# The first MLP in seven block products with transposed output, with one running sum and a reordered last group in both MLPs

## The chip, the cores and the metric

The kernel runs on one core of a Trainium2 chip. TensorE (PE) multiplies, VectorE (DVE), ScalarE (ACT) and GpSimd (POOL) work elementwise, SyncE (SP) and POOL issue the DMAs used here. The metric is the device time of one execution in microseconds; the median of several runs counts.

## The reference

A trunk of two layers over 512 tokens of 1024 channels, all float32. Layer 0 mixes tokens with a gated DeltaNet, layer 1 with a Conformer convolution. Each layer then attends into a fixed memory of 256 rows and applies an MLP:

```python
h = h + memory_cross_attention(rms_norm(h, xa_norm[layer]), ...)
h = h + sq_relu_mlp(rms_norm(h, mlp_norm[layer]), mlp_w_up[layer], mlp_w_down[layer])

def sq_relu_mlp(h, w_up, w_down):
    return jnp.square(jax.nn.relu(h @ w_up)) @ w_down
```

`w_up` is 1024 x 4096 and `w_down` 4096 x 1024. The result goes through a last RMSNorm.

## The kernel before

**Precision.** Every matmul operand is held as two parts in a fast 32-bit type: a rounded head and the remainder. A product of two such operands takes three matmuls (head x head, head x remainder, remainder x head). For weights, ACT writes the head `wh` from the loaded tile and DVE (in a few places POOL) the remainder `wl`, in `wsplit`; for activations `split` or `Norm.parts` does so. `Norm.add(t, h)` takes tile t of the residual: ACT scales it to `xh`, DVE makes `xl`, ACT squares it, POOL (for the last tile DVE) adds the squares. `norm.stat` sums the squares over the channels with two matmuls; ACT's root and DVE's reciprocal of 3.35 us give `rb`, by which the results are scaled when they are read from PSUM.

**Layout.** The residual is held transposed: 8 tiles of 128 channels x 512 tokens. `proj` computes 128 output channels for all tokens: 8 blocks of the contraction, three matmuls each, so 24 matmuls of 128 x 512, with the weights stationary.

**First MLP (`mlp`).** The 4096 hidden channels are taken in four groups of 1024. A group has 8 up projections and 8 down projections of 24 matmuls, in the order of `MLP_ORDER`. Each down result is added by DVE to the residual; in the last group this sum also reorders the tokens (`by_phase`, `phased`: token 4t+s goes to place s*128+t, as the convolution wants them), and `nxt.add` prepares the tile for the Conformer's norm at once. `mid`, called ahead of the last group, prepares the memory for layer 1 (`mem_gain`) and loads convolution taps.

**Second MLP (`mlp7`).** The down product of a group is a product of 2 x 2 blocks (halves of the tokens, halves of the hidden channels, halves of the output), and is done in seven block products instead of eight. The activations' blocks and their combinations (`early`, `late`: "11", "R3", "S1", "12", "R2", "S4", "22") are stationary and the weights' blocks move, so the result comes out with tokens on the partitions. The combined weight blocks are made by DMA: T3 and T1 are loaded and added to by accumulating DMAs on POOL's queue, T1's buffer (`T7`, of the three buffers `fs`) becomes T2 and later T4 by a further accumulation after each has been split (`after7`). Each product is 24 matmuls: 2 halves of 128 tokens, 4 blocks of the contraction, three matmuls. `evict` adds the results by DVE to eight accumulators (2 token halves x 2 output halves x 2), which in the first group have been filled with the turned residual by `turn` (32 PE transposes). Two more, "m" and "b", hold sums that belong to several outputs, and are given to them in the last group. `final` applies the last norm and writes the output.

**What sets the order.** The program is written in the order of the stages; a scheduler that knows durations then places instructions in each engine's queue, also earlier than they were written where buffers allow. Every engine works through its queue in order. `order`, `loads` and `need` plan the weights: each half weight tile (128 x 1024) is loaded by SP some units ahead (`wnext`: `NRAW` + 1, and two more from shortly ahead of the second MLP on) into six buffers `raw`, and split up to three units ahead (`NW`). 69 slots of 128 x 512 (`NSLOT`) hold the activations, 8 PSUM banks the results, 6 buffers `cv` the convolutions' inputs, three buffers `fs` the DeltaNet's solver, the convolution's inputs and the blocks T1.

**The Conformer's beginning.** `pw_mm` runs 16 projections (pairs m, half 0 and 1); the norm's statistics stand in the second of them, after its second contraction block. `pw_ev` then applies the gate. The convolution of pair 0 runs on ACT and POOL (`pool_conv`), of pairs 1 to 4 on DVE (`dve_conv`), of 5 to 7 on PE. Layer 1's memory projections fill PE beside them; POOL also splits some of these weights.

Of the kernel before, what the change touches and what calls it, by code (L numbers as in the profile page):

```python
# [14 lines left out]
P = 128  # L15
# [22 lines left out]
def tile_trunk(ctx, tc, xT, memT, x_d, mem_d, prm_d, adt_d, bdw_d, tap_d, fin_d, w_ab, w_kq, w_v, w_z, w_dno, w_pw1, w_pw2,  # L38
# [131 lines left out]
    def plan_mlp(layer):  # L170
        for kind, g in MLP_ORDER:
            for i in range(4):
                plan((kind, layer, g * 4 + i), (w_up if kind == "up" else w_dn)[layer, g * 4 + i])

    base7, sums7 = {}, set()
# [4 lines left out]
    def plan_mlp7(layer):  # L180
        for g in range(4):
            for i in range(4):
                plan(("up", layer, g * 4 + i), w_up[layer, g * 4 + i])
            n, base7["u", g] = len(loads), len(order)
            for b, h in LOADS7:
                if b == "T1":
                    sums7.add(len(loads))
                loads.append([block(layer, g, c, h) for c in PARTS7.get(b, [b])])
            for u in range(14):
                order.append((("dn7", g), u))  # L190
                bh = (ORDER7[u // 2][1], u % 2)
                need.append(n + LOADS7.index(bh) if bh in LOADS7 else need[-1])

# [9 lines left out]
    plan_mlp(0)  # L203
# [31 lines left out]
    def wsplit():  # L235
# [5 lines left out]
        raw = combos7(1, i, hf) if kind == "dn7" else ws["raw"].pop(need[u])  # L241
# [13 lines left out]
        if kind == "dn7":  # L255
            after7(1, i, hf)
# [13 lines left out]
    def combos7(layer, g, u):  # L270
        name, h = ORDER7[u // 2][1], u % 2
        if name in ("T2", "T4"):
            return T7[h]
        t = ws["raw"].pop(need[u + base7["u", g]])
        if name == "T1":
            T7[h] = t
        return t

    def after7(layer, g, u):
        name, h = ORDER7[u // 2][1], u % 2  # L280
        if name in ("T1", "T2"):
# [664 lines left out]

    def xattn(layer, norm, hres, nxt):
# [67 lines left out]
        def o_ev(m, ps):  # L1015
            hn = slot(s="h")
            tt(dve, hn, ps, hres[m], ALU.add)
# [38 lines left out]
    def mlp(layer, norm, hres, nxt, mid):  # L1056
        xs = norm.xs
        hid = {}
        cur = list(hres)
        st = {"first": []}  # L1060

        def up_ev(g, i, ps):
# [4 lines left out]
            hid.setdefault(g, []).append(split(u, "u"))  # L1067

        for kind, g in MLP_ORDER:
            if (kind, g) == ("dn", 3):  # L1070
                mid()
            for i in range(8):
                w = wnext((kind, layer, g * 4 + i // 2), i % 2)
                ps = psum(kind)
                if kind == "up":
                    proj(w, xs, ps, inside={1: norm.stat} if (g, i) == (0, 1) else None)
                    if g == 0 and i < 2:
                        st["first"].append(ps)
                        if i == 1:
                            for j in range(2):  # L1080
                                up_ev(0, j, st["first"][j])
                    else:
                        up_ev(g, i, ps)
                else:
                    proj(w, hid[g], ps)
                    hn = slot(s="h")
                    if g == 3:
                        tt(dve, by_phase(hn), phased(ps), phased(cur[i]), ALU.add)
                        nxt.add(i, hn)
                    else:  # L1090
                        tt(dve, hn, ps, cur[i], ALU.add)
                    cur[i] = hn
        return cur

    def phased(t):
        return t.rearrange("p (t s) -> p s t", s=4)  # L1100

    def by_phase(t):
        return t.rearrange("p (s t) -> p s t", s=4)
# [11 lines left out]
    def conformer(norm, hres, nxt):  # L1115
# [409 lines left out]
    h = mlp(0, n2, h, n3, lambda: (mem_gain(1, 0), mem_gain(1, 1), taps(NTAP)))  # L1525
    n4 = Norm("xa_norm1")
    h = conformer(n3, h, n4)
# [3 lines left out]

    def mlp7(layer, norm, hres):
        xs = norm.xs
        acc, first = {}, []
        gt = []

        def turn(i):
            n, m, c = i // 4, i // 2 % 2, i % 2
            ps, a = psum("hT"), slot(s="acc")
            for j in range(4):  # L1540
                pe.transpose(ps[:, j * P:(j + 1) * P], hres[4 * m + j][:, n * 256 + c * P:n * 256 + c * P + P], ident)
            act.copy(a, ps)
            acc[n, m, c] = a

        def up_ev(ps):
            t = slot(s="rl")
            stt(t, ps, 0.0, norm.rb, ALU.max, ALU.mult)
            u = slot(s="u2")
            act.activation(u, t, AF.Square)
            return u  # L1550

        def pair(t):
            return [t[0][:, 0:256], t[1][:, 0:256]], [t[0][:, 256:512], t[1][:, 256:512]]

        def early(o, u0):
            tt(dve, u0[:, 256:512], u0[:, 256:512], u0[:, 0:256], ALU.subtract)
            o["11"], o["R3"] = pair(split(u0, "a"))

        def late(o, u0, u1):
            x, y, r = slot(s="s12"), slot(s="s4"), slot(F32R, "s4")  # L1560
            tt(dve, x[:, 256:512], u1[:, 256:512], u0[:, 256:512], ALU.subtract)
            tt(dve, x[:, 0:256], u0[:, 0:256], x[:, 256:512], ALU.subtract)
            o["S1"], o["R2"] = pair(split(x, "s"))
            o["12"], o["22"] = pair(split(u1, "a"))
            tt(dve, y[:, 0:256], u1[:, 0:256], x[:, 256:512], ALU.subtract)
            act.copy(r[:, 0:256], y[:, 0:256])
            tt(dve, r[:, 256:512], y[:, 0:256], r[:, 0:256].bitcast(F32), ALU.subtract)
            o["S4"] = [r[:, 0:256], r[:, 256:512]]

        def dn7(g, ops):  # L1570
            bank = {}

            def part(left, w, ps, c, h, opens):
                for kk in range(2):
                    k, s = 2 * h + kk, slice(kk * 512, kk * 512 + 512)
                    xh, xl = [t[:, c * P:(c + 1) * P] for t in ops[k][left]]
                    pe.matmul(ps, xh, w[0][:, s], start=opens and k == 0, stop=False, skip_group_check=True)  # L1577
                    pe.matmul(ps, xl, w[0][:, s], start=False, stop=False, skip_group_check=True)  # L1578
                    pe.matmul(ps, xh, w[1][:, s], start=False, stop=k == 3, skip_group_check=True)  # L1579

            def product(i):
                left, right, key, opens = ORDER7[i]
                if opens:
                    bank[key] = [psum("dn") for _ in range(2)]
                ws_ = [wnext(("dn7", g), 2 * i)]
                if (g, i) == (3, 6):
                    ws_.append(wnext(("dn7", g), 13))
                    todo = [(0, 0), (0, 1), (1, 0), (1, 1)]
                else:
                    todo = [(0, 0), (1, 0), (0, 1), (1, 1)]  # L1590
                for c, h in todo:
                    if h == len(ws_):
                        ws_.append(wnext(("dn7", g), 2 * i + 1))
                    part(left, ws_[h], bank[key][c], c, h, opens)
                    if h == 1:
                        evict(right, c, bank[key][c])

            def into(key, c, ps, op=ALU.add):
                k = key + (c,)
                if k not in acc:  # L1600
                    acc[k] = slot(s="acc")
                    act.copy(acc[k], ps)
                else:
                    tt(dve, acc[k], acc[k], ps, op)
                return acc[k]

            def evict(right, c, ps):
                last = g == 3
                if right == "11":
                    m = into(("m",), c, ps)  # L1610
                    if last:
                        into((0, 0), c, m)
                        into(("b",), c, m, ALU.subtract)
                elif right == "T3":
                    into((0, 1), c, ps, ALU.subtract)
                elif right == "T1":
                    into((1, 1), c, ps)
                elif right == "21":
# [217 lines left out]
```

## Time and profile before

| | us |
|---|---|
| median of 3 runs | 1485.57 (1485.07 to 1485.91) |
| profiled execution | 1487.96 |
| its span | 1486.0 |
| first MLP, first up matmul to the Conformer's first matmul | 475.17 to 823.82 |
| second MLP, first up matmul to PE's end | 1145.16 to 1475.85 |
| PE's end to the end of the span | 10.15 |

The page gives the busy time of each engine and the chain of work that ended last. A table of stretches gives each engine's busy time in a window of the span. A row of the timeline has start, duration, engine, line, operation, output and inputs, and in brackets how long the engine stood idle before it and what ended that. Matmuls overlap, so the spacing of their starts is their price, not their duration. A group row has the count, then the busy time and the mean in ns of one, then the idle time before and its releasers. An operation that goes through a helper has the helper's line (`L69` is `tt`, `L72` is `stt`, `L78` is `ts`), so the tile's name tells more than the line.

### The profile page before, as it was taken

The numbers are of one execution on the slowest core, as the hardware profiler recorded it, in microseconds if no ns is written. First come the engines' busy times: TensorE is split into PE (matmuls) and PEld (weight loads), VectorE is DVE, ScalarE is ACT, GpSimd is POOL, SyncE is SP. The second block draws the span as 40 slices with busy tenths as digits, with TensorE's granted clock in tenths as the row PEclk, the third lists the DMA queues.
The fourth block names the chain that finished last, engine by engine and source line by source line (L and its number), as shares of the span: only waits on it lengthen the run. The fifth ranks groups of instructions, "written<-read, shape, count | busy, mean of one in ns | idle before, by whom it ended". The sixth has DMA issues, their size and how long they took to land.

```text
span 1486.0 us, 19375 instructions
## 1 busy us (share of the span) xinstructions
PE 1472.0 (99%) x7362; PEld 1241.1 (84%) x7362; DVE 986.7 (66%) x1468; ACT 729.0 (49%) x1262; POOL 240.2 (16%) x255
## 2 busy tenths in 40 slices
PE   9999999999999999999999999999999999999997
PEld 7888889988888888888888889988888888888885
DVE  5889888867555543443436699984645766767677
ACT  6766865655444432332314555464444554434344
POOL 1411310103112000000002388302112000000000
PEclk9999999999999999999999999999999999999999
DMA  7232123432213332223224524652203467575634
GB/s 269 93 114 72 58 87 126 142 115 97 73 34 109 99 100 95 91 98 100 99 99 156 174 96 135 192 178 93 86 29 113 114 170 178 140 193 140 186 99 113
DMA packets 55821, 176.63 MB, mean 119 GB/s; under 512 B 6961, under 2 KB 9265, under 8 KB 55729
## 3 DMA queue, kind: packets, MB, share of 16 engines
q1 hardware_dynamic: 50688, 158.10, 32.0%
q0 software_dynamic: 4608, 16.78, 6.6%
q8 instruction: 58, 0.95, 0.3%
q10 hardware_dynamic: 432, 0.52, 0.1%
q14 instruction: 35, 0.28, 0.1%
HBM read 172.49 MB, written 2.10 MB: 117 GB/s over the span
## 4 chain that ended last, share of the span: by engine, by line
PE 94%; DVE 3%; ACT 2%; issue 1%; DMA 1%; POOL 0%; SPq 0%; DVEq 0%
PE up L288 8%; PE up L287 8%; PE up L286 8%; PE dn L287 4%; PE dn L288 4%; PE dn L286 4%; PE dn L1578 3%; PE dn L1579 3%; PE dn L1577 3%; PE pw L288 3%; PE pw L287 3%; PE pw L286 3%; PE h L286 3%; PE h L287 2%; PE h L288 2%; PE xo L287 2%
## 5 line engine op out<-in xcount | busy, mean ns | idle before, releaser
L245 ACT CAST wh<-raw 128x1024 fp32r<-128x1024 f32 x255 | 267.7, 1051 | 498.1 <-PE up L287 133.7
L69 DVE TENSOR_TENSOR wl<-raw,wh 128x1024 fp32r<-128x1024 f32 (+1 forms) x246 | 303.7, 1236 | 93.7 <-ACT wh L245 87.6
L286 PE MATMUL up<-xh,wh 128*128 128x512 f32 x512 | 199.7, 390 | 0.0
L288 PE MATMUL up<-xh,wl 128*128 128x512 f32 x512 | 199.3, 389 | 0.0
L287 PE MATMUL up<-xl,wh 128*128 128x512 f32 x512 | 199.2, 389 | 0.0
L69 POOL TENSOR_TENSOR sq<-sq,sq 128x512 f32<-128x512 f32 x30 | 49.3, 1643 | 468.0 <-ACT sq L379 457.7
L72 DVE SCALAR_TENSOR_TENSOR rl<-up,rb 128x512 f32<-128x512 f32 x64 | 44.2, 691 | 106.0 <-PE up L288 105.9
L287 PEld LDWEIGHTS up<-xl,wh 128*128 128x128 f32 x512 | 96.1, 188 | 19.9
L286 PEld LDWEIGHTS up<-xh,wh 128*128 128x128 f32 x512 | 96.1, 188 | 19.9
L288 PEld LDWEIGHTS up<-xh,wl 128*128 128x128 f32 x512 | 96.1, 188 | 19.9
L286 PE MATMUL dn<-uh,wh 128*128 128x512 f32 x256 | 99.6, 389 | 0.0
L287 PE MATMUL dn<-ul,wh 128*128 128x512 f32 x256 | 99.6, 389 | 0.0
L288 PE MATMUL dn<-uh,wl 128*128 128x512 f32 x256 | 99.6, 389 | 0.0
L69 DVE TENSOR_TENSOR h<-dn,h 128x512 f32<-128x512 f32 x32 | 25.2, 788 | 91.5 <-PE dn L288 91.5
L1192 DVE SCALAR_TENSOR_TENSOR ca<-x,prm,ca 128x512 f32<-128x512 f32 x112 | 82.3, 753 | 3.6 <-ACT ca L1189 1.3
L286 PE MATMUL h<-xh,wh 128*128 128x512 f32 x184 | 73.7, 400 | 0.0
L288 PE MATMUL h<-xh,wl 128*128 128x512 f32 x184 | 71.9, 391 | 0.0
L287 PE MATMUL h<-xl,wh 128*128 128x512 f32 x184 | 71.7, 390 | 0.0
L286 PEld LDWEIGHTS dn<-uh,wh 128*128 128x128 f32 x256 | 48.0, 188 | 10.1
L287 PEld LDWEIGHTS dn<-ul,wh 128*128 128x128 f32 x256 | 48.0, 188 | 9.9
L288 PEld LDWEIGHTS dn<-uh,wl 128*128 128x128 f32 x256 | 48.0, 188 | 9.9
L72 DVE SCALAR_TENSOR_TENSOR cva<-cv,prm,cva 128x512 f32<-128x512 f32 x60 | 48.2, 830 | 11.4 <-POOL cva L69 10.3
(392 smaller groups left out, 3488.5 us busy)
## 6 DMA issues: line engine op xcount, KB each, us to landing
raw<-w_up SPq DMA_DIRECT2D x64, 512.0 KB, 3.5
raw<-w_dn SPq DMA_DIRECT2D x64, 512.0 KB, 3.5
raw<-w_pw SPq DMA_DIRECT2D x24, 512.0 KB, 3.6
t<-w_dn POOLq DMA_DIRECT2D x24, 512.0 KB, 5.6
raw<-w_k SPq DMA_DIRECT2D x16, 512.0 KB, 3.6
raw<-w_vv SPq DMA_DIRECT2D x16, 512.0 KB, 3.9
raw<-w_q SPq DMA_DIRECT2D x16, 512.0 KB, 3.4
raw<-w_o SPq DMA_DIRECT2D x16, 512.0 KB, 3.6
```

The costliest lines, as they stand in the source:

```text
L69: return e.tensor_tensor(out=o, in0=a, in1=b, op=op)
L72: return dve.scalar_tensor_tensor(out=o, in0=a, scalar=s, in1=b, op0=op0, op1=op1)
L245: ins = [act.copy(h, raw)]
L286: pe.matmul(ps, wh, xh, start=first, stop=False)
L287: pe.matmul(ps, wh, xl, start=False, stop=False)
L288: pe.matmul(ps, wl, xh, start=False, stop=last)
L1192: first["tap"] = dve.scalar_tensor_tensor(out=a, in0=src, scalar=w, in1=a, op0=ALU.mult, op1=ALU.add)
L1577: pe.matmul(ps, xh, w[0][:, s], start=opens and k == 0, stop=False, skip_group_check=True)
L1578: pe.matmul(ps, xl, w[0][:, s], start=False, stop=False, skip_group_check=True)
L1579: pe.matmul(ps, xh, w[1][:, s], start=False, stop=k == 3, skip_group_check=True)
```

## The change

- `mlp` is gone; `mlp7` serves both layers. In layer 0 it takes no `turn`: its accumulators start from the first result that reaches them (an ACT copy, negated where the result is to be subtracted), and the residual is added at the end. `outs` transposes the accumulators back, four output tiles with 16 PE transposes, adds the residual on DVE and calls `nxt.add`. Tiles 0 to 3 are done ahead of the last product of the last group, tiles 4 to 7 from inside the Conformer's first projection (`rest`).
- `pw_mm` does the first pair of projections in halves of the contraction: first half of projection 0, `rest`, first half of projection 1, second half of 0, second half of 1, with `norm.stat` in the last.
- The token order is changed in `o_ev` of layer 0's attention, so that the whole first MLP runs on reordered tokens.
- "m" and "b" become one running sum "p"; product "21" accumulates in the PSUM banks that product "11" opened, so that five opened pairs of banks become four.
- The last group of both layers runs in the order of `LAST7`: T2 directly after T1, and T2 is then loaded anew in three parts instead of being made from T1. Its buffer becomes T4.
- `BLOCKS7`, and with it the output halves, change places. Six of the ten accumulators (`ACC_CV`) lie in the `cv` buffers.
- Weights are loaded two units further ahead for all `up` and `dn7` units.

```diff
-LOADS7 = [(_b, _h) for _b in ("11", "T3", "T1", "21", "22") for _h in range(2)]
...
+            loads7 = [(o[1], h) for o in order7(g) if o[1] != "T4" and (g == 3 or o[1] != "T2") for h in range(2)]
...
-        while ws["load"] <= need[min(i + NRAW + 1 + 2 * (i > base7["u", 0] - 8), len(order) - 1)]:
+        while ws["load"] <= need[min(i + NRAW + 1 + 2 * (order[i][0][0] in ("up", "dn7")), len(order) - 1)]:
...
-            tt(dve, hn, ps, hres[m], ALU.add)
+            if layer == 0:
+                tt(dve, by_phase(hn), phased(ps), phased(hres[m]), ALU.add)
+            else:
+                tt(dve, hn, ps, hres[m], ALU.add)
...
+            def product(i):
+                if (layer, g, i) == (0, 3, 6):
+                    outs(range(4))
...
+                if k not in acc:
+                    acc[k] = acc_tile(key)
+                    act.activation(acc[k], ps, AF.Copy, scale=1.0 if op == ALU.add else -1.0)
...
+                elif right == "T2":
+                    p = into(("p",), c, ps, ALU.subtract)
+                    if last:
+                        into((1, 1), c, p, ALU.subtract)
+                        final(1, 1, c, True)
+                        into((0, 1), c, p, ALU.subtract)
+                        into((1, 0), c, p)
...
+        def outs(tiles):
+            todo = [(n, c, i) for n in range(2) for c in range(2) for i in tiles]
+            pss = {i: psum("hT") for i in tiles}
+            for n, c, i in todo:
+                j = 2 * n + c
+                pe.transpose(pss[i][:, j * P:(j + 1) * P], acc[n, 1 - i // 4, c][:, i % 4 * P:i % 4 * P + P], ident)
+            for k, i in enumerate(tiles):
+                hn = slot(s="h")
+                tt(dve, hn, pss[i], hres[i], ALU.add)
+                new[i] = hn
+                if k:
+                    nxt.add(i - 1, new[i - 1])
+            nxt.add(i, hn)
...
-            st[m, hf] = psum("pw")
-            proj(wnext(("pw1", m), hf), xs, st[m, hf], inside={1: norm.stat} if (m, hf) == (0, 1) else None)
+            w, st[m, hf] = wnext(("pw1", m), hf), psum("pw")
+            if m:
+                return proj(w, xs, st[m, hf])
+            proj(w, xs, st[m, hf], 0, 4)
+            if hf == 0:
+                st["w"] = w
+                return rest()
+            proj(st.pop("w"), xs, st[0, 0], 4, 8)
+            proj(w, xs, st[0, 1], 4, 8, inside={5: norm.stat})
...
-BLOCKS7 = ["11", "21", "12", "22"]
-PARTS7 = {"T3": ["12", "22"], "T1": ["12", "11"]}
+BLOCKS7 = ["12", "22", "11", "21"]
+PARTS7 = {"T3": ["12", "22"], "T1": ["12", "11"], "T2": ["22", "12", "11"]}
+ACC_CV = (("p",), (1, 0), (0, 0))
-ORDER7 = [("11", "11", "a", True), ("R3", "T3", "b", True), ("S1", "T1", "c", True), ("12", "21", "d", True),
+ORDER7 = [("11", "11", "a", True), ("R3", "T3", "b", True), ("S1", "T1", "c", True), ("12", "21", "a", False),
           ("R2", "T2", "b", False), ("S4", "22", "c", False), ("22", "T4", "e", True)]
+LAST7 = [ORDER7[_i] for _i in (0, 1, 2, 4, 5, 3, 6)]
```

More of the change, by code (lines that the diff above doesn't have):

```diff
@@ L168, in plan_x, with order7 @@
             plan(("xo", layer, h), w_o[layer, h])
[L170 to L173, printed above, removed]
     base7, sums7 = {}, set()
+    def order7(g):
+        return LAST7 if g == 3 else ORDER7
     def block(layer, g, b, h):
@@ L202, in tile_trunk @@
     plan_x(0)
-    plan_mlp(0)
+    plan_mlp7(0)
     for i in range(8):
@@ L1053, in xattn, with mlp7, acc_tile, turn @@
         return new
-    def mlp(layer, norm, hres, nxt, mid):
+    def mlp7(layer, norm, hres, nxt=None, mid=None):
         xs = norm.xs
[L1058 to L1062, printed above, removed]
+        acc, first = {}, []
+        gt = []
+        def acc_tile(key):
+            if key in ACC_CV:
+                return wp.tile([P, 544], F32, tag="cv", name=nm("acc"), bufs=NCV)[:, 0:NT]
+            return slot(s="acc")
+        def turn(i):
+            n, m, c = i // 4, i // 2 % 2, i % 2
+            ps, a = psum("hT"), acc_tile((n, m))
+            for j in range(4):
+                pe.transpose(ps[:, j * P:(j + 1) * P], hres[4 - 4 * m + j][:, n * 256 + c * P:n * 256 + c * P + P], ident)
+            act.copy(a, ps)
+            acc[n, m, c] = a
+        def up_ev(ps):
             t = slot(s="rl")
@@ new lines, in final @@
+        def final(n, m, c, opens):
+            if layer == 0:
+                return
+            x = acc[n, m, c]
+            rows = slice(n * 256 + c * P, n * 256 + c * P + P)
+            gs = slice(512 - m * 512, 1024 - m * 512)
+            ss = small(1)
+            act.activation(slot(s="fq"), x, AF.Square, accum_out=ss)
+            if opens:
+                b, y = small(1), slot(s="y")
+                ts(dve, b, ss, 1.0 / 1024, ALU.mult, EPS, ALU.add)
+                tt(dve, y, x, gt[0][:, gs], ALU.mult)
+                fin[n, c] = y, b, gs
+                return
+            y1, b, gs1 = fin.pop((n, c))
+            sd, rc, y = small(1), small(1), slot(s="y")
+            act.activation(sd, ss, AF.Sqrt, bias=b, scale=1.0 / 1024)
+            dve.reciprocal(rc, sd)
+            act.activation(y1, y1, AF.Copy, scale=rc)
+            stt(y, x, rc, gt[0][:, gs], ALU.mult, ALU.mult)
+            (act if (n, c) == (1, 1) else nc.sync).dma_start(out=yT[rows, gs1], in_=y1)
+            nc.sync.dma_start(out=yT[rows, gs], in_=y)
@@ new lines, in mlp7 @@
+        for g in range(4):
+            ops, us = [{} for _ in range(4)], []
+            for i in range(8):
+                w = wnext(("up", layer, g * 4 + i // 2), i % 2)
+                ps = psum("up")
+                proj(w, xs, ps, inside={1: norm.stat} if (g, i) == (0, 1) else None)
+                first.append(ps)
+                if (g, i) == (0, 0):
+                    continue
+                while first:
+                    us.append(up_ev(first.pop(0)))
+                    if len(us) % 2:
+                        early(ops[len(us) // 2], us[-1])
+                    else:
+                        late(ops[len(us) // 2 - 1], us[-2], us[-1])
+                if (layer, g) == (1, 0) and i > 1:
+                    turn(i - 2)
+            if (layer, g) == (1, 0):
+                turn(6)
+                turn(7)
+            if g == 3 and mid:
+                mid()
+            if (layer, g) == (1, 3):
+                gt.append(fsp.tile([P, 1024], F32, tag="fs", name=nm("gt")))
+                nc.sync.dma_start(out=gt[0], in_=fin_d.partition_broadcast(P))
+            dn7(g, ops)
@@ L1105, in tile_trunk @@
+        return new, lambda: outs(range(4, 8))
     TAPS = {}
@@ L1113, in taps, with conformer @@
             TAPS[m].append(t)
-    def conformer(norm, hres, nxt):
+    def conformer(norm, hres, nxt, rest):
         xs = norm.xs
@@ L1524, in tile_trunk @@
     n3 = Norm("cv_norm")
[L1525 removed]
+    h, rest = mlp7(0, n2, h, n3, lambda: (mem_gain(1, 0), mem_gain(1, 1), taps(NTAP)))
     n4 = Norm("xa_norm1")
[L1527 removed]
+    h = conformer(n3, h, n4, rest)
     n5 = Norm("mlp_norm1")
     h = xattn(1, n4, h, n5)
[L1532 to L1618, printed above, removed]
[L1619 to L1687 removed]
@@ L1814, in _layout @@
     halves = [8 * g + m for g in range(4) for m in (0, 4, 1, 5, 2, 6, 3, 7)]
[L1815 to L1817 removed]
+    r["w_up"] = np.stack([_pack_a(np, i["mlp_w_up"][j], halves) for j in range(2)])
+    r["w_dn"] = np.stack([np.concatenate([_pack_b(np, i["mlp_w_down"][j][g * 1024:(g + 1) * 1024]) for g in range(4)]) for j in range(2)])
     return r
```

199 lines of the change are left out of this document (87 added, 112 removed).

## The prediction

> **What bounds the kernel now.** I read the page's engine shares and its chain first, then PE's waits, then a table of stretches cut at the borders of the two MLPs.
>
> ```profile
> PE 1472.0 (99%) x7362; PEld 1241.1 (84%) x7362; DVE 986.7 (66%) x1468; ACT 729.0 (49%) x1262; POOL 240.2 (16%) x255
> PE 94%; DVE 3%; ACT 2%; issue 1%; DMA 1%; POOL 0%; SPq 0%; DVEq 0%
> PE K L288 <- POOL wl L69: 1.1, 1, 1.1
> core 0: us, PE busy (x) PEld busy (x) DVE busy (x) ACT busy (x) POOL busy (x), PEclk, DMA share, GB/s
> 475.17:823.98 348.81, 348.81 (x1540) 288.82 (x1539) 158.76 (x179) 120.39 (x156) 8.98 (x6) 1.00 0.31 104
> 851.66:949.00 97.34, 97.34 (x595) 86.89 (x594) 95.10 (x139) 51.08 (x93) 72.34 (x45) 1.00 0.45 140
> 1145.16:1475.85 330.69, 330.69 (x1475) 273.61 (x1473) 232.90 (x322) 154.78 (x211) 25.23 (x29) 1.00 0.56 145
> 475.17 0.39 PE L286 MATMUL up<-xh,wh 128*128 128x512 f32 x1
> 823.82 0.39 PE L286 MATMUL pw<-xh,wh 128*128 128x512 f32 x1
> 1145.16 0.39 PE L286 MATMUL up<-xh,wh 128*128 128x512 f32 x1
> 1475.62 0.39 PE L1579 MATMUL dn<-wl,ah 128*128 128x512 f32 x1
> 1185.81 0.44 PE hT L1541 x4
> ```
>
> PE is the bound: 94% of the chain, and after the start-up its list of waits holds one entry, 1.1 us in the conformer, for a weight remainder split on POOL. The first MLP runs from its first up matmul (475.17) to the conformer's first (823.82): 348.65 us for 1536 matmuls and the two of the norm's sum, so 0.2267 us each (their 0.39 us overlap). No slack hides in it: what PE issues there is what the stage costs.
>
> The second MLP already works in seven products, and is the model for the new stage: 1440 matmuls, two for the norm and 32 transposes end at 1475.62 + 0.23 = 1475.85. At 0.2267 us the 1442 take 326.9, which leaves 3.8 us for the transposes; by the chain four take 0.44, so 32 take 3.5. It is dense too, although DVE is busy 70% there (232.90 of 330.69) against 46% in the first MLP. That answers whether DVE, ACT or the loads can feed such a stage: they do, at the full granted clock (PEclk 1.00).
>
> **The change part by part.** The order of the changed program shows 1344 `dn` matmuls in place of 1440, 32 more transposes, and 68 accumulating DMAs on POOL's queue in place of 32.
>
> *Products.* Per group, 8 projections of 24 matmuls become 7 products of 24: 4 x 24 = 96 fewer x 0.2267 = -21.8 us, all on the path. This rate is measured on both ways of feeding PE, weights stationary and activations stationary. The Trainium skill (TensorE: Matmul & The Clock Gate, "Back-to-back issue gap") gives N/2.4 + 2.5 ns for a warm matmul, 215.8 ns for 512 columns; by it the 96 would be worth 20.7 us, but the trace shows 226.7 and I take that.
>
> *Transposes.* The second MLP turns the residual before its down products; the first now turns the result back: 16 in front of the last product and 16 inside the conformer's first projection. 32 x 0.11 = +3.5 us, up to +3.8 by the stage sum. I take 3.5.
>
> *Feeding the stage.* Groups of instructions in the stage of the second MLP (the third line: of the first):
>
> ```profile
> L69 DVE TENSOR_TENSOR wl<-raw,wh 128x1024 fp32r<-128x1024 f32 x62 | 75.9, 1225 | 26.5 <-ACT wh L245 26.5
> L245 ACT CAST wh<-t 128x1024 fp32r<-128x1024 f32 x24 | 25.4, 1056 | 29.2 <-PE dn L1578 20.4 <-DMA t<-w_dn 4.2 <-PE dn L1579 3.8
> L72 DVE SCALAR_TENSOR_TENSOR ml<-mem,prm,mh 128x256 fp32r<-128x256 f32 x8 | 3.2, 479 | 0.0
> L69 DVE TENSOR_TENSOR acc<-acc,acc 128x512 f32<-128x512 f32 x10 | 6.6, 687 | 0.0
> ```
>
> 24 more weight halves are split (DVE 1.22, ACT 1.06 us each), combinations of the operands come in and 32 sums of the old stage go. The second MLP does the same work with no PE wait, so it costs nothing there. The first group opens its accumulators with ACT copies in place of DVE sums, which lightens DVE; six of the ten accumulators lie in buffers of the convolutions, which stand empty in both MLPs. The pair of PSUM banks that product 11 opens now stays open for product 21: three open pairs hold six of the eight banks, the last product takes the other two, and no next group needs more than these pairs give back one by one; nothing, at worst one sum of 0.69 us per group.
>
> One place is tighter: the 8 gain steps for the memory (0.48 us each, 3.2 us in all with overlap) now run on DVE just as the last group's first products are fed. Laid end to end with the durations of before, the remainder for the second weight block of T1 comes 0.5 us late: +0.5, bounds 0 and 3.2.
>
> *One running sum, last group reordered.* In the second MLP's last group, product 11 loses four DVE sums (0.69 us) and the fresh T2 has three parts to load, two of them on POOL. It is loaded while the group's up projections run, and T4 now has two products, not one, to wait for its update. On PE 0.
>
> *The end of the second MLP.*
>
> ```profile
> 1475.48 0.72 ACT y L1659
> 1477.37 0.72 ACT y L1659
> 1479.26 0.72 ACT y L1659
> 1481.15 0.75 DVE y L72
> 1476.15 0.68 DVE L69 TENSOR_TENSOR acc<-acc,dn 128x512 f32<-128x512 f32 x1
> ```
>
> After PE's end four closings follow each other on ACT and DVE every 1.89 us, and then the output leaves. In the new order the first two close after the sixth product, one product earlier; but DVE's program puts the last sum (ready at PE's end + 0.30) ahead of the second closing's reciprocal. So the second closing's scaling starts at about PE's end + 1.1, against 1477.37 - 1475.85 = 1.5 now, and two more follow at 1.89: -0.4 us, bounds -1.9 (one closing gone) and 0.
>
> *The border to the conformer.* Here the cover is new. Before, each of the last 8 projections was added, scaled and squared while the next ran (the first line is a sum in plain token order, in the attention before):
>
> ```profile
> 469.93 0.69 DVE L69 TENSOR_TENSOR h<-xo,h 128x512 f32<-128x512 f32 x1 [2.65 <-PE xo L288]
> 818.58 1.09 DVE L69 TENSOR_TENSOR h<-dn,h 128x512 f32<-128x512 f32 x1 [2.56 <-PE dn L288]
> 819.70 0.72 ACT L372 ACTIVATE xh<-h,prm 128x512 fp32r<-128x512 f32 x1 [0.25 <-DVE h L69]
> 820.33 0.62 ACT L379 ACTIVATE sq<-h 128x512 f32<-128x512 f32 x1
> 820.73 0.74 DVE L72 SCALAR_TENSOR_TENSOR xl<-h,prm,xh 128x512 fp32r<-128x512 f32 x1
> 821.09 1.52 POOL L69 TENSOR_TENSOR sq<-sq,sq 128x512 f32<-128x512 f32 x1 [3.92 <-ACT sq L379]
> 832.06 3.35 DVE L395 RECIPROCAL rb<-sd 128x512 f32<-128x512 f32 x1 [0.48 <-ACT sd L393]
> 851.66 4.71 DVE L1192 SCALAR_TENSOR_TENSOR ca<-x,prm,ca 128x512 f32<-128x512 f32 x6 [1.26 <-ACT ca L1189]
> ```
>
> Now they come in two bunches of four. Four tiles cost DVE 4 x (0.69 + 0.74) = 5.7 us and ACT 4 x (0.72 + 0.62) = 5.4. The first bunch has the last product's 5.4 us as cover, the second the two half projections at 2.7 each. Call PE's end of the last product 0. In the changed order, with these durations, the fourth tile of the first bunch is ready at +2.9, needed at about +2.7 with 16 transposes as filler; the second bunch is ready at +6.5, +7.8, +9.0 and +10.0, against needs from +7.2 on at 0.7 per tile, then interleaved with the other half. The norm's sum is complete at +13.9; its two matmuls stand inside the third projection, with filler. So PE is just covered, with about half a microsecond to spare. Without that cover the whole second bunch would stand open: bounds 0 and 5.7. I take +0.5, near the lower end.
>
> *The conformer.* It is the second tight place: DVE is busy 95.10 of 97.34 us from the first tap on. The reciprocal now ends at +18.5 where it ended at 832.06 + 3.35 - 823.82 = +11.6, but the first tap waits for projection 3, which ends later only by the transposes, so it starts at about +28.5 against 851.66 - 823.82 = +27.8. DVE's chain moves less than PE's own 1.8 us, so nothing is added. POOL's chain starts some 6 us later and has idle time before its next weight splits. From the transposes on, PE's order is the old one. The 1.1 us wait on POOL can move by its own size either way.
>
> *Earlier steps.* The token order is now changed in the first attention's last step: 8 sums of 1.09 in place of 0.69 us on DVE, hidden under projections of 5.4 us. Three loads of the first MLP's combined blocks go out in the DeltaNet stage on SP, with their accumulating DMAs on POOL, when the buffers come free; in place of three memsets there:
>
> ```profile
> 251.19 0.16 POOL L1141 MEMSET x<- 128x70 f32 x1 [5.22 <-DVE u L665]
> 259.99 2.52 POOL L69 TENSOR_TENSOR cva<-cva,cvq 128x512 f32<-128x512 f32 x2 [8.64 <-ACT cvq L544]
> t<-w_dn POOLq DMA_DIRECT2D x24, 512.0 KB, 5.6
> raw<-w_dn SPq DMA_DIRECT2D x64, 512.0 KB, 3.5
> ```
>
> The last buffer is free at 251.19, its load lands 3.5 later, the issue takes 0.9: 255.6, ahead of the POOL work at 259.99. Nothing.
>
> **Sum:** -21.8 + 3.5 + 0.5 - 0.4 + 0.5 = -17.7 us. The profiled execution took 1487.96 us for a span of 1486.0 and lies 2.4 above the median of 1485.57; the sum is a difference of spans, so 1485.57 - 17.7 = 1467.9.
>
> **The rivals.**
>
> *The border stands open.* The bunches arrive late, by some added latency per step, and PE waits through most of the second bunch: up to 5.7 us, and 1 to 2 more in the conformer, whose DVE has no slack to catch up. 1469.5 to 1475; take 1472. For it: half a microsecond of cover. Against: the schedule interleaves transposes and the third projection as filler.
>
> *The accumulating DMAs become the bound (slower).* Each group's T1 buffer is split, updated to T2, split, updated to T4, split, all through POOL's queue.
>
> ```profile
> 1457.16 1.05 ACT L245 CAST wh<-t 128x1024 fp32r<-128x1024 f32 x1 [1.80 <-DMA t<-w_dn]
> 1458.24 1.23 DVE L69 TENSOR_TENSOR wl<-t,wh 128x1024 fp32r<-128x1024 f32 x1 [1.63 <-ACT wh L245]
> 1461.97 0.39 PE L1579 MATMUL dn<-wl,sh 128*128 128x512 f32 x1
> ```
>
> Even where ACT waits for such an update, DVE is done at 1459.47 and PE takes that block from about 1462.0: 2.5 us of slack. The first MLP has 14 such updates (two per half of the block in three groups, one in the last). To eat 17.7 us each must stall PE 1.3 us, so land 3.8 us later than it does now, at a median of 5.6; from there on the kernel is slower, and at 5 us later it would take 1485.57 - 17.7 + 14 x 2.5 = 1502.9. The second MLP does the same at 70% DVE load with no PE wait. The Trainium skill (SBUF — State Buffer, "SBUF: two separate sides") says that a DMA issued from GpSimd needs GpSimd to write its descriptors, and that this is locked out while VectorE runs certain operations, so that the transfer looks blocked. The median landing of 5.6 against 3.5 on SP's queue fits that, but no PE wait follows from it here.
>
> *More is gained.* The POOL wait in the conformer goes and one closing at the end vanishes: -1.1 and -1.5 more, 1465.3.
>
> *The change doesn't do what it says.* The 96 matmuls are gone from the program; only another bound could hide that, and DVE at 70% isn't one.
>
> **How the numbers follow.** As forecast (1466.5 to 1469.5): 0.60. Border open: 0.25. More gained: 0.10. Slower: 0.04; rest, no change, 0.01. Leaving out the slower case and the far end of the open border, the range is 1465.3 to 1473.0. A change of 0.2% (3 us) is about what can be told from none; all but 0.05 lies on the faster side.
>
> **What would show it.** Right: first up to first `pw` matmul falls from 348.65 to about 329 (326.9 for 1442 matmuls, 1.8 for 16 transposes, 0.5); groups of `dn` at 1344 matmuls; PE's waits still a microsecond or two. Wrong: PE waits on `xl` or the transposes at the conformer's start, PE `dn` waiting for ACT `wh` behind a DMA, or POOL's wait for the K block growing.

## The result and the profile after

The changed kernel takes 1476.7 us (median of 4 runs, 1473.81 to 1479.44); the kernel before took 1485.74 beside it. The ratio is 0.9939, with a 95% interval of 0.992 to 0.9959. It is faster, by about 9.0 us, but half of the forecast 17.7 us is missing, and 1476.7 lies outside the range of 1465.3 to 1473.0. The profiled execution took 1477.09 us for a span of 1475.4.

The page of the changed kernel (engine shares; shares of the chain), and then PE's waits after the start-up (in total, times, longest):

```profile
PE 1458.1 (99%) x7298; PEld 1228.4 (83%) x7298; DVE 1071.9 (73%) x1614; ACT 770.8 (52%) x1326; POOL 270.2 (18%) x291
PE 90%; DVE 4%; ACT 2%; DMA 1%; issue 1%; POOL 1%; SPq 0%; POOLq 0%; ACTq 0%; DVEq 0%
```

```profile
PE K L288 <- POOL wl L69: 3.3, 1, 3.3
...
PE pw L287 <- DVE xl L72: 1.1, 3, 0.6
...
PE dn L1117 <- DVE wl L69: 0.2, 1, 0.2
```

PE is still the bound, but its share of the chain fell from 94% to 90%, and two waits are new or longer: one in the memory projections (`K`, 3.3 us where 1.1 stood) and three on `xl` where the Conformer begins.

The time is found by cutting at matmuls that both kernels have. The first matmul of each stage, after and then before (start, duration; the other starts of before stand in the prediction):

```profile
474.33 0.39 PE L286 MATMUL up<-xh,wh 128*128 128x512 f32 x1
...
803.51 0.39 PE L286 MATMUL pw<-xh,wh 128*128 128x512 f32 x1
...
904.63 0.28 PE L286 MATMUL K<-mh,wh 128*128 128x256 f32 x1
...
951.08 0.48 PE L319 MATMUL V<-wh,mh 128*128 128x512 f32 x1
...
1134.65 0.39 PE L286 MATMUL up<-xh,wh 128*128 128x512 f32 x1
...
1465.46 0.39 PE L1117 MATMUL dn<-wl,ah 128*128 128x512 f32 x1
```

```profile
919.95 0.28 PE L286 MATMUL K<-mh,wh 128*128 128x256 f32 x1
...
961.61 0.48 PE L319 MATMUL V<-wh,mh 128*128 128x512 f32 x1
```

| stretch (us) | before | after | moved | forecast |
|---|---|---|---|---|
| start to first `up` | 475.17 | 474.33 | -0.84 | 0 |
| first MLP, to first `pw` | 348.65 | 329.18 | -19.47 | -19.5 |
| first `pw` to first `K` | 96.13 | 101.12 | +4.99 | +2.3 |
| first `K` to first `V` | 41.66 | 46.45 | +4.79 | 0 |
| first `V` to second `up` | 183.55 | 183.57 | +0.02 | 0 |
| second MLP, to the last matmul | 330.46 | 330.81 | +0.35 | 0 |
| last matmul to the end of the span | 10.38 | 9.94 | -0.44 | -0.4 |

The sum is -10.6, the difference of the two profiled spans; the medians differ by 9.0, and the times of the changed kernel spread over 5.6. (The -19.5 is the forecast's -21.8 + 1.8 + 0.5: half of the transposes stand in front of the first `pw`.) The first MLP came out as forecast. The loss sits in two places of the Conformer: 2.7 us more than forecast around its beginning, 4.8 in the K projections.

**The K projections.** Timeline of PE at the wait, and a table of stretches over it (PE, PEld, DVE, ACT, POOL busy with counts, then PEclk, DMA share, GB/s), after:

```profile
938.90 0.28 PE L287 MATMUL K<-ml,wh 128*128 128x256 f32 x1
942.51 0.58 PE L288 MATMUL K<-mh,wl 128*128 128x256 f32 x1 [3.34 <-POOL wl L69]
```

```profile
934.00:938.00 4.00, 4.00 (x36) 4.00 (x35) 3.75 (x5) 1.97 (x6) 3.85 (x4) 1.00 0.96 210
938.00:942.00 4.00, 1.18 (x10) 0.97 (x9) 3.96 (x4) 1.53 (x2) 3.99 (x2) 0.96 0.62 119
942.00:944.00 2.00, 1.49 (x7) 1.49 (x8) 2.00 (x2) 0.00 (x0) 0.46 (x1) 0.50 0.26 78
944.00:946.00 2.00, 2.00 (x11) 2.00 (x11) 1.56 (x3) 0.00 (x0) 0.00 (x0) 0.50 0.98 320
946.00:948.00 2.00, 2.00 (x11) 2.00 (x11) 0.00 (x0) 0.55 (x1) 0.00 (x0) 0.50 0.95 373
948.00:950.00 2.00, 2.00 (x17) 2.00 (x16) 1.48 (x2) 0.49 (x1) 0.00 (x0) 0.88 0.07 25
```

PE stands for 3.34 us, and then the granted clock is 0.50 until about 948: 11 matmuls in 2 us where the clock at 1.00 gives 18 (36 in 4 us). The busy time hides this, because a slow matmul counts as busy. Why POOL is late is seen on the queues: SP's after, POOL's after, and SP's before:

```profile
912.45 12.51 SPq L1302 DMA_DIRECT2D xg<-glu  x16
...
925.68 0.38 SPq L227 DMA_DIRECT2D t<-w_dn  x1
```

```profile
930.79 0.89 POOL L233 DMA_DIRECT2D t<-w_dn  x1 [8.33 <-DMA t<-w_dn]
931.40 4.36 POOL L69 TENSOR_TENSOR cb<-cb,cvp 128x512 f32<-128x512 f32 x3
935.73 0.88 POOL L233 DMA_DIRECT2D t<-w_dn  x1
936.35 3.82 POOL L69 TENSOR_TENSOR cb<-cb,cvp 128x512 f32<-128x512 f32 x2
940.12 2.34 POOL L69 TENSOR_TENSOR wl<-raw,wh 128x1024 fp32r<-128x1024 f32 x1
```

```profile
925.39 0.70 SPq L227 DMA_DIRECT2D t<-w_dn  x1
926.40 14.24 SPq L1153 DMA_DIRECT2D xg<-glu  x16
```

The second MLP's T1 is fetched already here: SP loads a part, POOL adds the second part to it by an accumulating DMA. POOL cannot issue that before the load has landed, and all behind it waits: five sums `cb` of the convolution (8.2 us) and then the remainder `wl` that PE needs. In the kernel before SP issued the load at 925.39, ahead of the last convolution inputs `xg`; now it comes behind sixteen of them, whose issue takes 12.5 us, while the K projections come 15 us earlier (904.63 against 919.95).

**The border.** Timeline of DVE and of POOL after the last product, which ends at 803.5 (start, duration):

```profile
803.63 1.79 DVE L72 SCALAR_TENSOR_TENSOR xl<-h,prm,xh 128x512 fp32r<-128x512 f32 x1
805.34 1.27 DVE L69 TENSOR_TENSOR acc<-acc,dn 128x512 f32<-128x512 f32 x2
806.53 0.74 DVE L72 SCALAR_TENSOR_TENSOR xl<-h,prm,xh 128x512 fp32r<-128x512 f32 x1
807.20 2.30 DVE L69 TENSOR_TENSOR wl<-raw,wh 128x1024 fp32r<-128x1024 f32 x1
...
810.89 0.75 DVE L72 SCALAR_TENSOR_TENSOR xl<-h,prm,xh 128x512 fp32r<-128x512 f32 x1 [0.20 <-ACT xh L372]
811.56 0.68 DVE L69 TENSOR_TENSOR h<-hT,h 128x512 f32<-128x512 f32 x1
812.16 1.21 DVE L72 SCALAR_TENSOR_TENSOR xl<-h,prm,xh 128x512 fp32r<-128x512 f32 x1
...
813.89 2.88 DVE L72 SCALAR_TENSOR_TENSOR xl<-h,prm,xh 128x512 fp32r<-128x512 f32 x2
```

```profile
802.62 2.25 POOL L69 TENSOR_TENSOR sq<-sq,sq 128x512 f32<-128x512 f32 x1 [6.55 <-ACT sq L379]
805.25 3.16 POOL L69 TENSOR_TENSOR sq<-sq,sq 128x512 f32<-128x512 f32 x2 [0.38 <-ACT sq L379]
...
811.52 4.70 POOL L69 TENSOR_TENSOR sq<-sq,sq 128x512 f32<-128x512 f32 x3 [2.99 <-ACT sq L379]
```

`xl` took 0.74 us in the kernel before and `wl` 1.21; here, where they start while POOL adds squares, they take 1.79 and 2.30. Two `xl` that start shortly ahead of a POOL sum keep their time (806.53, where the second sum of the row `x2` starts at 806.64, and 810.89, ahead of 811.52). The sums that read one operand from PSUM (`acc`, `h`) keep their 0.6 to 0.7.

### The profile page after: what moved, and what is told of

Same layout as the page of the kernel before. It is cut to its first block, busy times and chain, and to the rows that moved or that the text cites. A ratio compares the mean times of both kernels' runs of the same rounds, so it can differ in the third digit from the quotient of the medians.

```text
span 1475.4 us, 19619 instructions
## 1 busy us (share of the span) xinstructions
PE 1458.1 (99%) x7298; PEld 1228.4 (83%) x7298; DVE 1071.9 (73%) x1614; ACT 770.8 (52%) x1326; POOL 270.2 (18%) x291
## 4 chain that ended last, share of the span: by engine, by line
PE 90%; DVE 4%; ACT 2%; DMA 1%; issue 1%; POOL 1%; SPq 0%; POOLq 0%; ACTq 0%; DVEq 0%
PE up L287 8%; PE up L288 8%; PE up L286 8%; PE dn L1117 7%; PE dn L1115 7%; PE dn L1116 7%; PE pw L287 3%; PE pw L288 3%; PE pw L286 3%; PE h L286 2%; PE h L287 2%; PE h L288 2%; PE xo L287 2%; PE xo L286 2%; PE q L287 2%; PE q L288 2%
## 5 line engine op out<-in xcount | busy, mean ns | idle before, releaser
L245 ACT CAST wh<-raw 128x1024 fp32r<-128x1024 f32 x259 | 271.4, 1050 | 362.9 <-issue 100.9
L69 DVE TENSOR_TENSOR wl<-raw,wh 128x1024 fp32r<-128x1024 f32 (+1 forms) x250 | 309.5, 1240 | 106.4 <-ACT wh L245 98.8
L233 POOL DMA_DIRECT2D t<-w_dn x48 | 41.9, 873 | 406.8 <-DVE wl L69 218.4
L1115 PE MATMUL dn<-wh,ah 128*128 128x512 f32 x256 | 100.0, 391 | 0.1
L1116 PE MATMUL dn<-wh,al 128*128 128x512 f32 x256 | 99.5, 389 | 0.0
L1117 PE MATMUL dn<-wl,ah 128*128 128x512 f32 x256 | 99.2, 389 | 0.0
L245 ACT CAST wh<-t 128x1024 fp32r<-128x1024 f32 x44 | 46.3, 1052 | 57.0 <-PE dn L1116 46.1
L69 DVE TENSOR_TENSOR wl<-t,wh 128x1024 fp32r<-128x1024 f32 x44 | 53.8, 1225 | 30.4 <-ACT wh L245 30.3
L69 DVE TENSOR_TENSOR acc<-acc,dn 128x512 f32<-128x512 f32 x100 | 67.5, 683 | 2.4 <-PE dn L1117 1.2
L69 DVE TENSOR_TENSOR al<-u,ah 128x512 fp32r<-128x512 f32 x64 | 44.1, 689 | 21.4 <-ACT ah L325 21.4
```

What stands on the lines that cost most here:

```text
L69: return e.tensor_tensor(out=o, in0=a, in1=b, op=op)
L233: nc.gpsimd.dma_start(out=t, in_=a, accum_op=ALU.add)
L245: ins = [act.copy(h, raw)]
```

## The experiments

The theory after these readings: (a) POOL's queue, held by the accumulating DMA, makes PE wait in the K projections; (b) that wait also lowers PE's clock behind it; (c) at the border DVE's steps are lengthened by POOL's sums. The rival: the Conformer's DVE chain is late from the border on (it was busy for 95 of 97 us before), so PE would be held there in any case.

**e1: the late remainder on DVE.**

```diff
-        gp = kind == "pw1" and 2 * i + hf > 6 or j and kind == "K" and i == 1 and hf == 0
+        gp = kind == "pw1" and 2 * i + hf > 6 or j and kind == "K" and i == 1 and hf == 0 and j[0] < 3
```

> The changed kernel, but the remainder of the K block for which TensorE waits 3.3 us (the last of the four that GpSimd makes) is made on VectorE. Theory (GpSimd's queue): GpSimd comes late to this block because two accumulating transfers of the second MLP's T1 stand ahead of it and wait for their load; so TensorE's wait of 3.3 us in the K projections goes, and with it the half clock (0.50) of the 4 us behind it; K projections cost what they cost before the change. About 3.3 + 2 us less: 1471.5, between 1470.5 and 1473. Rival (the Conformer's VectorE chain is late from the border on, 95 of 97 us busy, and TensorE would be held anyway): another wait of 2 us or more stands in the same stretch, on VectorE, and the time stays at 1475 or above.

Measured: 1470.72 us (1469.72 to 1471.72), ratio to before 0.9901 (0.9886 to 0.9916). PE has no K wait any more, and first `K` to first `V` takes 40.26 us: 6.2 less than after, 1.4 less than before the change.

**e2: the accumulating transfers held back.** The split stays on POOL; only the queue's order changes.

```diff
-        nc.gpsimd.dma_start(out=t, in_=a, accum_op=ALU.add)
+        with tc.issue_after(ws["gp"].ins) if "gp" in ws else nullcontext():
+            nc.gpsimd.dma_start(out=t, in_=a, accum_op=ALU.add)
...
+        if gp:
+            ws["gp"] = ins[1]
```

> The changed kernel, but the accumulating transfers of the second MLP's first blocks are queued on GpSimd behind the last split of a K block; all else stays. Theory (GpSimd's queue): GpSimd's 21.7 us of waiting for their loads falls away ahead of the split, the split is done some 8 us earlier, the wait of 3.3 us for it and the half clock behind it go: 1471.5, between 1470 and 1473, the same as with the split on VectorE. Rival (GpSimd is late because of its own sums, or VectorE's chain is late): a wait for this split of over 1.5 us stays, 1475 or above.

Measured: 1470.77 us (1469.56 to 1472.59), ratio 0.9903 (0.9888 to 0.9917); first `K` to first `V` 40.27. PE's waits of this kernel after the start-up are all that is left:

```profile
PE pw L290 <- DVE xl L72: 1.1, 3, 0.6
PE dn L1120 <- DVE wl L69: 0.2, 1, 0.2
```

Two different ways to free the split give the same gain, 6.0 and 5.9 us against 1476.7. The rival falls: no wait on DVE takes the place of the one removed. The second MLP takes 330.76, so the transfer, issued at 934.79 in place of 930.79, costs nothing there.

**e3: no sums of squares on POOL.** It leaves out six of the seven sums of the Conformer's norm.

```diff
-            else:
+            elif self.n == KT or self.g != "cv_norm":
                 tt(dve if self.n == KT else pool, self.acc, self.acc, sq, ALU.add)
```

> The changed kernel without the six sums of squares on GpSimd for the Conformer's norm (this leaves part of the norm's sum out). Theory (VectorE is slowed while GpSimd adds): the eight xl steps at the border go back from 0.97 to about 0.74 us and the weight remainder there from 2.30 to 1.23; of the 2.9 us that TensorE loses between the last product and the fourth projection about 2 go, so 1474.5 if the K wait stays as it is. Rival (VectorE simply has too many steps there, or the chain transposes, sum, scaling is too long): the durations or at least TensorE's waits stay, 1476 to 1477.

Measured: 1472.4 us (1471.79 to 1474.54), ratio 0.9916 (0.9899 to 0.9932). The timeline of DVE, the same steps as above:

```profile
803.12 0.75 DVE L72 SCALAR_TENSOR_TENSOR xl<-h,prm,xh 128x512 fp32r<-128x512 f32 x1
...
805.92 1.22 DVE L69 TENSOR_TENSOR wl<-raw,wh 128x1024 fp32r<-128x1024 f32 x1
...
810.34 0.74 DVE L72 SCALAR_TENSOR_TENSOR xl<-h,prm,xh 128x512 fp32r<-128x512 f32 x1
...
811.60 1.63 DVE L72 SCALAR_TENSOR_TENSOR xl<-h,prm,xh 128x512 fp32r<-128x512 f32 x2
```

The four rows together are 3.8 us shorter, PE's waits on `xl` are gone, and first `pw` to first `K` falls from 101.12 to 98.86. So (c) holds, at 2.26 us. The time fell by 2 us more than expected; that came from the K projections (44.44 in place of 46.45), where the wait was 2.5 us instead of 3.3 and the half clock shorter.

**e4 and e10: the wait alone, in the kernel before.** The same remainder is made twice in a row on POOL, whole (e4; for e10 columns 0 to 511 only).

```diff
+        if gp and (kind, *j, hf) == ("K", 3, 0):
+            tt(pool, lo, raw, h.bitcast(F32), ALU.subtract)
         ins.append(tt(pool if gp else dve, lo, raw, h.bitcast(F32), ALU.subtract))
```

> The kernel before the change, but the same K remainder is made twice in a row on GpSimd, so that TensorE's wait of 1.1 us there becomes about 3.5 us, as long as in the changed kernel. If only the wait itself costs: +2.4 us, 1488. If a wait of that length also lowers TensorE's granted clock behind it: +2.4 and another 2 to 2.5 us, 1490 to 1490.5, with a granted clock near 0.5 in the 4 us behind the wait.

> The kernel before the change, with half of the K remainder made twice on GpSimd, so that TensorE's wait there is about 2.3 us. It asks from what length on a wait lowers the clock: waits that left 1.4 us between two matmul starts did not, 2.7 us did (the run without sums). If 2.3 us is enough: +1.2 us of wait and about 1.5 of clock, 1488.3, with a stretch at half clock behind it. If not: +1.2, 1486.8, and the clock stays at 1.00.

Measured: e4 1490.1 us (1488.37 to 1491.03), ratio to before 1.003 (1.0019 to 1.0042); e10 1487.52 (1484.12 to 1493.38), ratio 1.0015 (1.0003 to 1.0027). Stretches behind the wait, of e4 and then of e10 (the clock is the third number from the end):

```profile
956.00:958.00 2.00, 2.00 (x11) 2.00 (x11) 2.00 (x3) 0.00 (x0) 0.00 (x0) 0.50 0.63 215
958.00:960.00 2.00, 2.00 (x14) 2.00 (x13) 0.78 (x2) 0.00 (x0) 0.00 (x0) 0.64 0.89 322
960.00:962.00 2.00, 2.00 (x20) 2.00 (x19) 0.74 (x1) 1.05 (x1) 0.00 (x0) 1.00 0.66 250
```

```profile
956.00:958.00 2.00, 2.00 (x16) 2.00 (x17) 2.00 (x3) 0.00 (x0) 0.00 (x0) 1.00 0.49 172
958.00:960.00 2.00, 2.00 (x19) 2.00 (x18) 1.05 (x2) 1.05 (x1) 0.00 (x0) 1.00 0.86 315
```

In e4 PE waits 3.8 us in place of 1.1 (+2.7), and the time rises by 4.6: (b) holds, for a kernel that knows nothing of the change. In e10's profiled execution PE waits 2.0 us and the clock stays at 1.00. Its times spread over 9 us, so what a wait of that length costs in other executions stays open.

**e5 and e6: the sums on DVE.** Both hold the transfers (e2), and DVE adds the squares; in e5 where the scheduler puts them, in e6 all behind the last `xl` (`self.xl` is that step; the line with `issue_after` stands in e6 alone).

```diff
...
+            elif self.g == "cv_norm":
+                self.sums.append(sq)
+                if self.n == KT:
+                    with tc.issue_after(self.xl.ins):
+                        for s in self.sums:
+                            tt(dve, self.acc, self.acc, s, ALU.add)
```

> The changed kernel with the accumulating transfers held behind the last K split, and with the six sums of squares of the Conformer's norm moved from GpSimd to VectorE, at the places where the scheduler puts them. Theory: the xl steps at the border take 0.74 us again, TensorE's loss there falls from 2.9 to about 1, while VectorE gets six sums of about 0.6 us (3.7 us) for 4.1 us of lengthening that go: 1469, between 1468 and 1470.5. Rival: the added sums delay the last xl or the norm's sum as much as the lengthening did: 1470.8 or more, as with the transfers held alone.

> As the run before, but all seven sums stand on VectorE behind the last xl step. Theory: the xl steps come as early as with no sums at all, TensorE's waits for xl vanish, but the norm's sum comes after seven sums and two weight remainders, about 6.6 us behind the last xl, near the place where TensorE takes it, so up to 1 us there: 1468.5 to 1470. Rival: TensorE waits for the norm's sum by over 2 us: above 1470.8.

Measured: e5 1470.23 us (1469.09 to 1470.74), ratio 0.9892 (0.9876 to 0.9907), not to be told from e2. e6 1476.05 (1474.39 to 1476.63), ratio 0.9932 (0.992 to 0.9945), 5.3 slower than e2. `xl` takes 0.74 us in both, but PE now waits for the norm's sum, 1.0 us in e5 and 5.3 in e6. PE's wait and the stretches around it, e6:

```profile
PE ssq L400 <- ACT sqh L328: 5.3, 1, 5.3
```

```profile
816.00:820.00 4.00, 0.76 (x4) 0.30 (x2) 3.62 (x5) 1.35 (x2) 0.00 (x0) 1.00 0.34 126
820.00:824.00 4.00, 1.94 (x4) 1.31 (x5) 2.02 (x3) 0.99 (x2) 0.00 (x0) 0.62 0.37 136
824.00:828.00 4.00, 4.00 (x12) 3.09 (x11) 3.62 (x2) 1.59 (x2) 0.00 (x0) 0.53 0.00 0
```

The rival came true: a new wait took the place, and the slow clock followed it here too (12 matmuls in 4 us where 18 fit), in another stage.

**e7 and e8: the norm's matmuls one projection later.** e6 (for e7) and e5 (for e8), with `norm.stat` in the third projection in place of the second, and `pw_ev(0)` behind it.

```diff
-                return proj(w, xs, st[m, hf])
+                return proj(w, xs, st[m, hf], inside={5: norm.stat} if (m, hf) == (1, 0) else None)
...
-            proj(w, xs, st[0, 1], 4, 8, inside={5: norm.stat})
+            proj(w, xs, st[0, 1], 4, 8)
...
-                if hf == 1:
+                if (m, hf) == (1, 0):
+                    pw_ev(0)
+                if hf == 1 and m:
                     pw_ev(m)
```

> The kernel of e6 (transfers held, sums on VectorE behind the last xl), with the norm's two matmuls one projection later (in the third, contraction block 5), so 5.4 us further on. Theory: e6 lost 5.3 us by TensorE's wait for the norm's sum and more by the half clock behind it; both go, xl stays early, and the border costs what it did without any sums (98.9 us from the first pw matmul to the first K matmul, against 101.1): 1468.5, between 1467.5 and 1470. Rival: the later reciprocal makes VectorE's taps late, which has 95 busy of 97 us, and a wait turns up in the K or V projections: 1470.8 or more.

> The kernel of e5 (transfers held, sums on VectorE where the scheduler puts them), with the norm's two matmuls one projection later. Theory: e5's 1.0 us wait for the norm's sum goes, xl is a little later than in e7: 1469, between 1468 and 1470. Rival: as for e7.

Measured: e8 1468.15 us (1468.03 to 1468.57), ratio 0.9885 (0.9871 to 0.9898): the best of all, 8.6 us below the change. First `pw` to first `K` takes 98.64, first `K` to first `V` 40.27, and PE's largest wait after DeltaNet is 0.2 us. e7 1471.82 (1470.56 to 1473.87), ratio 0.9908 (0.9895 to 0.9922): its border is as good, PE is busy for every microsecond from 796 to 828, but the convolution on POOL starts later (832.96 against 830.39 in e8), and POOL's queue makes PE wait once more, now for a `pw` remainder (first `pw` to first `K` 103.12):

```profile
PE pw L291 <- POOL wl L69: 2.9, 1, 2.9
```

Behind this wait, too, the granted clock is 0.50, from 859.00 to 862.42. So POOL, 2.6 us later, loses what DVE's order had gained.

**e9: without the half projections.** e2, with the last four tiles ahead of the whole first projection.

```diff
-            proj(w, xs, st[m, hf], 0, 4)
             if hf == 0:
-                st["w"] = w
-                return rest()
-            proj(st.pop("w"), xs, st[0, 0], 4, 8)
-            proj(w, xs, st[0, 1], 4, 8, inside={5: norm.stat})
+                rest()
+            proj(w, xs, st[m, hf], inside={5: norm.stat} if hf else None)
```

> The kernel with the transfers held (e2), but the first two projections of the Conformer whole again and the last four tiles transposed and scaled ahead of the first: the cover of the second bunch is taken away. The first projection then meets the tiles 4 to 7 after 4 contraction blocks (2.7 us) instead of 5.4. If the half projections are worth their length, TensorE waits 2 to 3 us more at the border and its clock falls behind it: 1473 to 1476. If they are worth nothing: 1470.8.

Measured: 1470.65 us (1469.6 to 1471.85), ratio 0.9901 (0.9888 to 0.9915), as e2; first `up` to first `K` takes 430.26 against 430.30. The second branch of the expectation came true, because the scheduler makes the filler itself. It places four matmuls of the first projection between the two groups of eight transposes, and lets the first two projections alternate while the last tiles arrive. What is written as halves buys nothing.

## Why the prediction was wrong

- **Products, transposes ahead of the last product, feeding the stage: right.** -19.5 forecast, -19.47 measured. The rate of 0.2267 us, the 1.8 us for 16 transposes and the 0.5 for the late remainder stand as a sum. PE waits for that remainder at 775.25; by the starts around it (774.71 to 775.59, two spacings) this costs 0.43.
- **The border: right mechanism, wrong size.** Forecast +0.5 beside 1.8 for transposes; measured 4.99 - 1.8 = 3.2. The sum used `xl` at 0.74 us, a row that starts 0.36 us ahead of POOL's sum (820.73 against 821.09). With four tiles in a bunch, DVE's steps start while POOL's sums run, and they lengthen by 3.8 us. Without the sums 2.26 of the 3.2 go (e3), with the sums on DVE and the norm later 2.5 (e8). The rival "the border stands open" named the place but not this reason.
- **The conformer: the step that failed.** "DVE's chain moves less than PE's own 1.8 us, so nothing is added" was right in effect, as e2 has no wait on DVE there, but not in size: the first tap starts at 835.18, 31.7 us behind the first `pw`, where 28.5 was forecast and 27.8 stood before. "POOL's chain starts some 6 us later and has idle time before its next weight splits" failed. It starts 10.2 us later (27.2 behind the first `pw` against 17.0), which alone makes no wait (e2: 27.2 too). But 8.33 us of the idle time is the wait of an accumulating DMA for its load, and the queue puts that DMA ahead of the split. The forecast bounded the 1.1 us wait "by its own size either way"; it grew by 2.2, and the half clock behind it, for which the sum has no term, took the rest, together 4.8 us. That the wait for the K block could grow stood among the signs of being wrong, without a price.
- **The end: right**, -0.44 for -0.4. The second MLP is 0.35 longer where 0 was forecast, and 0.3 to 0.4 in every kernel built on the change. The matmul starts show the place: at 1455.56 and 1455.90 two follow 0.44 and 0.34 us behind the one before, against 0.23 for matmuls in a row, where PE takes a weight head `wh` that ACT ends at 1455.51. The same two spacings stand in all nine kernels with the change and not in the kernel before; why ACT is late there stays open. The 0.84 ahead of the first `up` is no effect: that start varies from 472.58 (e4) to 475.17 (before) among kernels that do the same up to there.
- **The rivals.** "The accumulating DMAs become the bound" looked for late landings in the MLP; what cost time was an issue that waits on POOL, in another stage. "More is gained" was right that the POOL wait could go: e2 takes 40.27 for the K projections, 1.4 less than the kernel before.

With both causes treated (e8) the time is 1468.15, where 1467.9 was forecast. But e8 holds an extra gain of 1.4 in the K projections, which pays for the 0.7 left at the border (98.64 against 96.13 + 1.8) and the second MLP's 0.35; that the two numbers nearly meet is luck. Beside the kernel before of its own session (1484.96) e8 gains 16.8 us, not 17.7.

## What to carry to other kernels

When a stage gets shorter, look at what each in-order queue holds behind it, and above all at prefetches for much later that wait on an engine with work due now. A duration read from a row holds only for the neighbours that it had there: work that is bunched runs beside other engines. A wait of about three microseconds on TensorE cost 1.5 to 1.9 times its length here: 3.34 us became 6.2 (after against e1), 2.9 became 4.5 (e7 against e8).

## What was not expected of the hardware

**A wait lowers PE's clock behind it.** In one profiled execution each, 1.42 us (before) and 2.32 us (e10) between two matmul starts left the clock at 1.00, while 2.74 us (e3), 3.27 (e7), 3.61 (after), 4.10 (e4) and 5.69 (e6) lowered it to 0.50. By the traces' records of the granted clock it then stays low for 3.41 us (e3, e4, e7) or for 6.83 us, twice as long (after, e6). The matmuls of 256 columns follow each other at 0.21 us in this stretch, in place of 0.12. The length of the slow stretch does not follow the length of the wait. It was single where PE was running again when the clock fell (e3: 1.44 us behind the restart) and double where PE still stood (after: the clock falls at 941.64, PE restarts at 942.51). The Trainium skill (TensorE: Matmul & The Clock Gate, "What's actually happening") has the clock halve after an idle window of about 3.4 us and return after as long a busy one, with windows that run freely. The half clock and the two lengths agree with it; that 2.74 us were enough lies below its figure.

**DVE is slowed by POOL.** Steps with both tensors in SBUF (`xl`, `wl`) that start while a sum of POOL runs are lengthened by 0.4 to 1.1 us each; those that start ahead of it are not (0.74 and 0.75 us at 806.53 and 810.89), nor those with one tensor in PSUM (0.6 to 0.7 us for `h` and `acc`). The Trainium skill (SBUF — State Buffer, "Who interferes with whom") says just this: a VectorE instruction with two SBUF inputs and a GpSimd instruction that reads SBUF exclude each other. The trace agrees, and the prediction should have drawn on it.
